# Padding the small on-chip tiles so that every large tile begins at a multiple of 128 bytes

## The chip, the cores and the metric

The kernel runs on one core of a Trainium2 chip. The metric is the device time of one execution in microseconds. A core has a matrix engine (PE, whose loads of the stationary operand are listed apart as PEld), a vector engine (DVE), a scalar engine (ACT), a general engine (POOL) and a sync engine (SP), from whose queue all transfers of this kernel are issued. On-chip memory (SBUF) has 128 partitions; a tile takes the same byte range in each of them, and it is the first byte of this range that the change moves.

## The reference, cut to what matters

The reference is a small transformer in float32: 256 tokens, width 1024. One block has a gated feed-forward, a mixer that joins sparse attention and a gated linear recurrence, and a second gated feed-forward. Two more blocks follow, each with a feed-forward, a mixer (forgetting attention, then latent attention), a feed-forward and a gated embedding. Nearly all work is products of a 256-row activation with weights that are read once:

```python
def swiglu(x, w_gu, w_down):
    gate, up = jnp.split(x @ w_gu, 2, axis=-1)
    return (jax.nn.silu(gate) * up) @ w_down
...
for l in range(DEPTH):
    h = h + 0.5 * swiglu(rms_norm(h, ffn1_norm[l]), ffn1_w_gu[l], ffn1_w_down[l])
    h = h + hybrid_mixer(rms_norm(h, mix_norm[l]), w_in[l], ...)
    h = h + 0.5 * swiglu(rms_norm(h, ffn2_norm[l]), ffn2_w_gu[l], ffn2_w_down[l])
```

## The kernel before, in words

The 256 tokens are two tiles of 128 rows, T = 0 and T = 1. A generator `net(T)` writes out the program of each; `run` steps the two in turn, T = 1 some steps behind, so that one weight serves both soon after each other. The order of instructions on each engine is fixed when the program is built.

**Weights.** `load_unit` issues the transfer of a weight block of 128 x 512 floats into a tile `wr` (6 buffers). ACT rounds it to the PE's fp32r format (L318, tile `w`), and DVE takes the rest that the rounding lost (L319, another tile `w`; 42 buffers in all).

**Products.** `mm3` makes one float32 product from three fp32r matmuls (L347 to L349): the high part of the activation with the high and with the low part of the weight, then the low part of the activation with the high part of the weight. The weight tile `w` is the moving operand and streams through PE (mostly 512 columns); a 128 x 128 piece of the activation (`xh`, `xl` or a working tile `s`) is the stationary operand, and is loaded anew for each matmul. In the rows below `mm<-w,xh` reads: written `mm` in PSUM, moving `w`, stationary `xh`. Two kinds of matmul have it otherwise. At L1198 to L1200 the weight `w` is stationary and the activation `keep` moves, in 256 columns. At L766 the moving operand is a weight again, in plain float32 (two passes, so two instructions, for one product), and the stationary operands are pieces of 30 columns of one tile `s`, each 120 bytes behind the one before.

**Small tiles.** Scalars per row (`col`, a ring of 26 slots; `sc`, `rq`, `gt`) hold statistics and gates. The reciprocal square root of a norm is POOL's power operation (L454 and L544), with a constant column `mhalf` as its exponent.

**Placing.** Tiles are placed in SBUF in the order in which they are first asked for. First come `x0`, the `wr` and the `w` tiles, then the constants, `g1`, `x1`, `mhalf`, and then `xh`, `xl`, the 20 working tiles `s2` (`s` in the rows), `col`, `sc` and the rest. A tile begins at a multiple of 32 bytes, right behind the one before.

Of the kernel before, what the change touches and what calls it, by code (L numbers as in the profile page):

```python
# [11 lines left out]
FT = mybir.dt.float32  # L12
FR = mybir.dt.float32r
# [7 lines left out]
P = 128  # L21
# [242 lines left out]
class Net:  # L264
# [21 lines left out]
        return self.t("keep", [P, n, w], 5, dt)  # L286

    def col(self, n=1):
        return self.t("col", [P, n], 26)

    def pt(self, tag, cols=512):
        self.uid += 1
# [196 lines left out]

    def scales(self, vs):  # L490
        r = self.rstd(vs[0], 1e-6, extra=vs[1])
        sc = self.t("sc", [P, 2], 4)
        self.nc.vector.tensor_scalar(sc[:, 0:1], r, 0.5, None, op0=OP.mult)
        self.nc.vector.tensor_tensor(sc[:, 1:2], r, r, op=OP.mult)
        return sc
# [420 lines left out]
    def nsa_proj(self, T, xT, nsa):  # L916
        nc, sh, c = self.nc, self.sh, self.c
        if T == 0:
            for _ in range(8):
                yield "c1"  # L920
        else:
            yield from self.compress()
        pz = yield from self.dense("nq", xT, 4, 512)
        q = self.s2()
        nc.scalar.activation(q, pz, AF.Copy)
        tp = self.pt("tr")
        for i in range(4):
            self.tr(tp[:, P * i:P * i + P], q[:, P * i:P * i + P])
        nqT = self.s2().rearrange("p (i t) -> p i t", i=4)
        nc.vector.tensor_tensor(nqT, tp.rearrange("p (i t) -> p i t", i=4),  # L930
                                c["qsc"].unsqueeze(2).to_broadcast([P, 4, P]), op=OP.mult)
        nsa["q"] = nqT
        pz = yield from self.dense("vv", xT, 4, 280)
        nc.scalar.activation(sh["nv"][:, T, :], pz[:, 0:256], AF.Copy)
        gt = self.t("gt", [P, 24], 2)
        nc.scalar.activation(gt, pz[:, 256:280], AF.Tanh, scale=0.5)
        nc.vector.tensor_scalar(gt, gt, 0.5, 0.5, op0=OP.mult, op1=OP.add)
        nsa["g"] = gt
# [270 lines left out]
    def mla(self, T, xT, done):  # L1209
        nc, sh = self.nc, self.sh  # L1210
# [3 lines left out]
        with self.tc.high_priority(offset=HP):  # L1214
            q = self.s2()
            nc.vector.tensor_tensor(q[:, 0:384], pz[:, 0:384], self.gain("mla_q_norm_2")[:, 0:384], op=OP.mult)
            ms, junk = self.col(), self.s2()
            nc.scalar.activation(junk[:, 0:384], pz[:, 0:384], AF.Square, scale=384 ** -0.5, accum_out=ms)
            rq = self.rstd(ms, 1e-6, dst=self.t("rq", [P, 1], 2))
            tp = self.pt("tr")  # L1220
            for i in range(3):
                self.tr(tp[:, P * i:P * i + P], q[:, P * i:P * i + P])
            ch, cl = ((self.keep(P, 3, FR) if T == 0 else
                       self.s2(dt=FR)[:, 0:384].rearrange("p (k t) -> p k t", k=3)) for _ in range(2))
            self.split(ch, cl, tp[:, 0:384].rearrange("p (k t) -> p k t", k=3))
# [215 lines left out]


def late(n, nc, sb, a, vec, ct):
    nc.sync.dma_start(ct[:, P:], a["const"][:, P:])
    lf = n.s2()[:, 0:64 * len(LEVELS)]
    nc.sync.dma_start(lf, a["lvl"])
    n.lvl = sb.tile([P, 64 * len(LEVELS)], U8, name="lvl")
    nc.vector.tensor_copy(n.lvl, lf)
    n.c["cpos"] = sb.tile([P, 2, 16], FT, name="cpos")
    nc.sync.dma_start(n.c["cpos"], a["cpos"])  # L1450
    n.w2 = sb.tile([P, 2, 128], FT, name="w2")
    nc.sync.dma_start(n.w2, a["w2"])
    n.bf = sb.tile([P, 16], FT, name="bf")
    o, w = vec["fox_b_f_2"]
    nc.sync.dma_start(n.bf, a["vec"][o:o + w].rearrange("(o w) -> o w", o=1).broadcast_to([P, w]))
    for k in ("hgrn_out_norm", "kv_norm_2", "mla_q_norm_2"):
        o, w = vec[k]
        n.small[k] = sb.tile([P, w], FT, name=k)
        nc.sync.dma_start(n.small[k], a["vec"][o:o + w].rearrange("(o w) -> o w", o=1).broadcast_to([P, w]))
    n.fsel = sb.tile([P, 16], FR, name="fsel")  # L1460
    nc.scalar.activation(n.fsel, n.c["fsel"], AF.Copy)


def build(nc, tc, a, units, offs, coff, vec):
    with tc.tile_pool(name="sb", bufs=1) as sb, tc.tile_pool(name="ps", bufs=1, space=PSUM) as ps:
        n = Net(nc, tc, sb, ps, a, units, offs)
        n.vec = vec
        xs = []
        for T in range(2):
            x = sb.tile([P, D], FT, name=f"x{T}")  # L1470
            xs.append(x)
            if T == 0:
                n.preload(PRE)
                ct = sb.tile([P, a["const"].shape[1]], FT, name="const")
                nc.sync.dma_start(ct[:, 0:P], a["const"][:, 0:P])
                nc.sync.dma_start(x, a["x"][0:P, :])
                n.c["g1"] = sb.tile([P, 8], FT, name="g1")
                nc.sync.dma_start(n.c["g1"], a["g1"])
                n.x, n.small = xs, {}
        for k, (o, w) in coff.items():  # L1480
            n.c[k] = ct[:, o:o + w]
        n.c["mhalf"] = sb.tile([P, 24], FT, name="mhalf")
        nc.gpsimd.memset(n.c["mhalf"], -0.5)
        n.late = lambda: late(n, nc, sb, a, vec, ct)
        n.run()
# [43 lines left out]
```

## Time and profile before

| | |
|---|---|
| median of 3 runs | 1709.43 us (1705.27 to 1710.35) |
| profiled execution, device time | 1710.19 us |
| its span, first to last instruction | 1708.4 us |
| PE busy | 1678.5 us, 98% of the span |
| DVE busy | 1115.4 us, 65% |
| ACT busy | 937.5 us, 55% |
| POOL busy | 23.8 us, 1% |
| mean granted TensorE clock | 0.997 |

All times below are of the profiled execution. Busy time of PE runs from the start of a matmul to its modelled end, and ends overlap the next start, so the pace of PE is read from the starts that follow each other.

### The profile page before, as it was taken

The page shows a single profiled execution, that of the slowest core. Times are in us where ns is not written, and L with a number is a line of the kernel's source. Part 1 is how long each engine was busy: PE and PEld are TensorE (multiplying, and loading weights), DVE is VectorE, ACT ScalarE, POOL GpSimd, SP SyncE. Part 2 cuts the span into 40 slices and gives each one's busy share as a digit, 9 for nine tenths or more (in the row PEclk, how much of TensorE's full clock was granted, in tenths as well). Part 3 has the DMA queues.
Part 4 walks back from the last instruction along what each step waited for, and adds up shares of the span by engine and source line. Part 5 has one row for each costly group of instructions (what it writes and reads, how often), then busy time and mean ns, then how long its engine had stood idle before and what let it go on. Part 6 is the DMA issues. An engine that isn't in the chain of part 4 may idle for free.

```text
span 1708.4 us, 24828 instructions
## 1 busy us (share of the span) xinstructions
PE 1678.5 (98%) x8010; PEld 1346.2 (79%) x8010; DVE 1115.4 (65%) x2308; ACT 937.5 (55%) x1899; POOL 23.8 (1%) x43
## 2 busy tenths in 40 slices
PE   8999999999999999999999999999999999999997
PEld 6888776777888788878887888778888888788876
DVE  6655666666665766567557565785666865766666
ACT  7545665555555555556555555564555774555553
POOL 0000000000000000000000000000000000000000
PEclk9999999999999999999999999999999999999999
DMA  8755554336655566555436555575655633565652
GB/s 270 264 176 171 171 175 125 99 105 191 185 184 174 168 186 188 182 166 158 141 121 198 185 185 184 173 223 165 195 185 163 207 100 99 184 199 185 185 173 74
DMA packets 160402, 292.99 MB, mean 171 GB/s; under 512 B 18192, under 2 KB 27152, under 8 KB 160272
## 3 DMA queue, kind: packets, MB, share of 16 engines
q1 hardware_dynamic: 160272, 291.41, 55.0%
q8 instruction: 63, 1.03, 0.3%
q14 instruction: 67, 0.55, 0.1%
HBM read 290.29 MB, written 1.05 MB: 171 GB/s over the span
## 4 chain that ended last, share of the span: by engine, by line
PE 90%; DVE 4%; ACT 2%; issue 1%; DMA 1%; POOL 1%; SPq 0%; DVEq 0%; POOLq 0%; ACTq 0%
PE mm L347 16%; PE mm L348 16%; PE mm L349 16%; PE a L347 10%; PE a L348 10%; PE a L349 10%; PE tr L357 5%; PE a L766 1%; DMA wr<-wp 1%; DVE x L542 1%; DVE w L319 1%; DVE x L559 1%; PE a L989 1%; PE a L857 1%; PE a L1281 1%
## 5 line engine op out<-in xcount | busy, mean ns | idle before, releaser
L319 DVE TENSOR_TENSOR w<-wr,w 128x512 fp32r<-128x512 f32 (+3 forms) x1058 | 706.7, 680 | 369.6 <-ACT w L318 154.9
L318 ACT ACTIVATE w<-wr 128x512 fp32r<-128x512 f32 (+3 forms) x1058 | 648.7, 622 | 412.8 <-PE mm L348 240.9
L347 PE MATMUL mm<-w,xh 128*128 128x512 f32 (+3 forms) x1200 | 481.2, 401 | 0.0
L348 PE MATMUL mm<-w,xh 128*128 128x512 f32 (+3 forms) x1200 | 470.1, 392 | 0.0
L349 PE MATMUL mm<-w,xl 128*128 128x512 f32 (+3 forms) x1200 | 469.1, 391 | 0.0
L347 PEld LDWEIGHTS mm<-w,xh 128*128 128x128 f32 x1200 | 225.7, 188 | 49.0 <-issue 4.4
L349 PEld LDWEIGHTS mm<-w,xl 128*128 128x128 f32 x1200 | 225.6, 188 | 47.9
L348 PEld LDWEIGHTS mm<-w,xh 128*128 128x128 f32 x1200 | 226.3, 189 | 43.2 <-issue 0.6
L348 PE MATMUL a<-w,s 128*128 128x512 f32 x531 | 211.1, 398 | 0.0
L347 PE MATMUL a<-w,s 128*128 128x512 f32 x531 | 210.5, 396 | 0.5 <-ACT s L352 0.5
L349 PE MATMUL a<-w,s 128*128 128x512 f32 x531 | 209.8, 395 | 0.2 <-DVE s L353 0.2
L347 PEld LDWEIGHTS a<-w,s 128*128 128x128 f32 x531 | 99.6, 188 | 28.7 <-issue 4.1
L347 PE MATMUL a<-w,xh 128*128 128x512 f32 (+2 forms) x304 | 121.0, 399 | 0.8 <-ACT xh L352 0.7
L348 PE MATMUL a<-w,xh 128*128 128x512 f32 (+2 forms) x304 | 119.6, 394 | 0.0
L349 PE MATMUL a<-w,xl 128*128 128x512 f32 (+2 forms) x304 | 119.0, 394 | 0.0
L349 PEld LDWEIGHTS a<-w,s 128*128 128x128 f32 x531 | 99.6, 188 | 23.9 <-DVE s L353 0.6
L348 PEld LDWEIGHTS a<-w,s 128*128 128x128 f32 x531 | 99.7, 188 | 22.9
L352 ACT ACTIVATE s<-tr 128x256 fp32r<-128x256 f32 (+2 forms) x137 | 50.8, 372 | 74.9 <-PE tr L357 74.7
L353 DVE TENSOR_TENSOR s<-tr,s 128x256 fp32r<-128x256 f32 (+2 forms) x137 | 56.5, 413 | 50.8 <-ACT s L352 50.5
L357 PE MATMUL tr<-const,s 128*128 128x128 f32 (+1 forms) x436 | 77.6, 274 | 2.1 <-DVE s L471 1.4
L357 PEld LDWEIGHTS tr<-const,s 128*128 128x128 f32 (+1 forms) x436 | 56.2, 140 | 28.7 <-DVE s L471 2.7
L347 PEld LDWEIGHTS a<-w,xh 128*128 128x128 f32 x304 | 57.5, 189 | 15.6 <-ACT xh L352 3.3
(277 smaller groups left out, 1356.7 us busy)
## 6 DMA issues: line engine op xcount, KB each, us to landing
wr<-wp SPq DMA_DIRECT2D x994, 256.0 KB, 2.7
gb<-vec SPq DMA_DIRECT2D x21, 512.0 KB, 4.0
wr<-wp SPq DMA_DIRECT2D x32, 192.0 KB, 2.4
w<-wp SPq DMA_DIRECT2D x16, 256.0 KB, 4.8
wr<-wp SPq DMA_DIRECT2D x16, 160.0 KB, 2.4
wr<-wp SPq DMA_DIRECT2D x8, 168.0 KB, 2.3
wr<-wp SPq DMA_DIRECT2D x8, 140.0 KB, 2.2
x<-x SPq DMA_DIRECT2D x2, 512.0 KB, 6.2
```

The costliest lines, as they stand in the source:

```text
L318: nc.scalar.activation(hi[:, 0:w], r[:, 0:w], AF.Copy)
L319: nc.vector.tensor_tensor(lo[:, 0:w], r[:, 0:w], hi[:, 0:w].bitcast(FT), op=OP.subtract)
L347: mm(out, xh, wh, start=start, stop=False)
L348: mm(out, xh, wl, start=False, stop=False)
L349: mm(out, xl, wh, start=False, stop=stop)
L352: self.nc.scalar.activation(hi, src, AF.Copy)
L353: self.nc.vector.tensor_tensor(lo, src, hi.bitcast(FT), op=OP.subtract)
L357: self.nc.tensor.transpose(out, src, self.c["ident"][0:n, 0:n])
L542: nc.vector.scalar_tensor_tensor(y[:, cs], y[:, cs], nm, g[:, cs], op0=OP.add, op1=OP.mult)
L559: self.nc.vector.scalar_tensor_tensor(x[:, cs], acc, c, x[:, cs], op0=OP.mult, op1=OP.add, accum_out=s)
L766: nc.tensor.matmul(hp[0:2 * nb, 256 * kv:256 * kv + 256], kbs[kv][:, cc].rearrange("p g b -> p (g b)"), u[i][0], start=cc == 0, stop=cc == 15)
L857: nc.tensor.matmul(ap[:, 64 * h:64 * h + 64], k[:, P * h:P * h + P], dq[:, 64 * h:64 * h + 64], start=True, stop=True)
```

## The change

Small tiles are padded, or become columns of another tile. No instruction is added, removed or moved; addresses change. The ring `col` has 24 slots in place of 26. `g1` and `bf` become columns behind the constants, and `fsel` and `mhalf` share a tile `misc`; `sc`, `gt` and `rq` are padded.

```diff
     def col(self, n=1):
-        return self.t("col", [P, n], 26)
+        return self.t("col", [P, n], 24)
...
-        sc = self.t("sc", [P, 2], 4)
+        sc = self.t("sc", [P, 8], 4)
...
-        gt = self.t("gt", [P, 24], 2)
+        gt = self.t("gt", [P, 32], 2)[:, 0:24]
...
-            rq = self.rstd(ms, 1e-6, dst=self.t("rq", [P, 1], 2))
+            rq = self.rstd(ms, 1e-6, dst=self.t("rq", [P, 16], 2)[:, 0:1])
...
-    nc.sync.dma_start(ct[:, P:], a["const"][:, P:])
+    nc.sync.dma_start(ct[:, P:a["const"].shape[1]], a["const"][:, P:])
...
-    n.bf = sb.tile([P, 16], FT, name="bf")
...
-    n.fsel = sb.tile([P, 16], FR, name="fsel")
+    n.fsel = n.misc[:, 0:16]
...
-                ct = sb.tile([P, a["const"].shape[1]], FT, name="const")
+                nc0 = a["const"].shape[1]
+                ct = sb.tile([P, -(-(nc0 + 24) // 32) * 32], FT, name="const")
...
-                n.c["g1"] = sb.tile([P, 8], FT, name="g1")
+                n.c["g1"] = ct[:, nc0:nc0 + 8]
+                n.bf = ct[:, nc0 + 8:nc0 + 24]
...
-        n.c["mhalf"] = sb.tile([P, 24], FT, name="mhalf")
+        n.misc = sb.tile([P, 32], FR, name="misc")
+        n.c["mhalf"] = n.misc[:, 16:32].bitcast(FT)
```

Where the tiles begin, in bytes past a multiple of 128, as the two programs place them:

| tile | before | after |
|---|---|---|
| `x0`, all `wr`, all `w`, `const` | 0 | 0 |
| `x1` | 64 | 0 |
| `xh`, `xl`, `s2`, `keep`, `gb`, `lvl`, `w2` | 32 | 0 |
| `se`, `pT`, the gains `hgrn_out_norm`, `kv_norm_2`, `mla_q_norm_2` | 96 | 0 |
| `col` slots | 32 or 96 | 0 or 64 |

On SP, the first transfers of the program stand in the same places; `x_61` is `x0`, and `g` in the third row is the tile `g1`. Before:

```order
L1475 DMA const<-const 128x128
L1476 DMA x_61<-x 128x1024
L1478 DMA g_77<-g 128x8
L311 DMA wr_123<-wp 128x512
L311 DMA wr_125<-wp 128x512
```

and in the changed kernel:

```order
L1475 DMA const<-const 128x128
L1476 DMA x_61<-x 128x1024
L1479 DMA const<-g 128x8
L311 DMA wr_122<-wp 128x512
L311 DMA wr_124<-wp 128x512
```

The 4 KB of `g1` go to columns of `const`; nothing has changed its place in the queue.

On POOL, these are the power operations of the second feed-forward of the first block and of the layers behind it, with the engines that each waits for. Before:

```order
L454 TENSOR_TENSOR col_3913<-col_3913,mhalf 128x1 [waits DVE_49]
L454 TENSOR_TENSOR col_4040<-col_4040,mhalf 128x1 [waits DVE_49]
L454 TENSOR_TENSOR col_5779<-col_5779,mhalf 128x1 [waits DVE_49]
L454 TENSOR_TENSOR col_5962<-col_5962,mhalf 128x1 [waits DVE_49]
L544 TENSOR_TENSOR col_7689<-col_7689,mhalf 128x1 [waits DVE_49,Activation_49]
```

and in the changed kernel:

```order
L454 TENSOR_TENSOR col_3910<-col_3910,misc 128x1 [waits DVE_49,Pool_49]
L454 TENSOR_TENSOR col_4037<-col_4037,misc 128x1 [waits DVE_49]
L454 TENSOR_TENSOR col_5776<-col_5776,misc 128x1 [waits DVE_49,Pool_49]
L454 TENSOR_TENSOR col_5959<-col_5959,misc 128x1 [waits DVE_49]
L544 TENSOR_TENSOR col_7686<-col_7686,misc 128x1 [waits DVE_49,Activation_49]
```

The order is the same. Some of the operations name POOL itself as well, for the last use of a `col` slot that now comes round after 24 instead of 26. Over the whole program the waits of PE, DVE and SP are the same one for one; ACT has 4 separate wait instructions fewer and POOL 5 more.

## Rows read from the trace of the kernel before

**Rows 1.** The page: span, then an engine's busy time, share and instructions.

```profile
span 1708.4 us, 24828 instructions
PE 1678.5 (98%) x8010; PEld 1346.2 (79%) x8010; DVE 1115.4 (65%) x2308; ACT 937.5 (55%) x1899; POOL 23.8 (1%) x43
```

**Rows 2.** The page: chain of work that ended last, shares of the span.

```profile
PE 90%; DVE 4%; ACT 2%; issue 1%; DMA 1%; POOL 1%; SPq 0%; DVEq 0%; POOLq 0%; ACTq 0%
```

**Rows 3.** The page's costliest groups: busy us, mean ns, idle before, releaser.

```profile
L347 PE MATMUL mm<-w,xh 128*128 128x512 f32 (+3 forms) x1200 | 481.2, 401 | 0.0
...
L347 PE MATMUL a<-w,s 128*128 128x512 f32 x531 | 210.5, 396 | 0.5 <-ACT s L352 0.5
...
L347 PE MATMUL a<-w,xh 128*128 128x512 f32 (+2 forms) x304 | 121.0, 399 | 0.8 <-ACT xh L352 0.7
```

**Rows 4.** Timeline of PE, 512 columns: start, duration; ten matmuls, first and last.

```profile
400.15 0.39 PE L348 MATMUL mm<-w,xh 128*128 128x512 f32 x1
...
402.25 0.39 PE L348 MATMUL a<-w,xh 128*128 128x512 f32 x1
```

**Rows 5.** Timeline of PE, 320 columns: eight starts, first and last.

```profile
816.67 0.31 PE L349 MATMUL mm<-w,xl 128*128 128x320 f32 x1
...
817.70 0.39 PE L347 MATMUL mm<-w,xh 128*128 128x512 f32 x1
```

**Rows 6.** Timeline of PE, weight stationary, 256 columns: 22 starts, first and last.

```profile
1320.36 0.28 PE L1198 MATMUL mm<-keep,w 128*128 128x256 f32 x1
...
1322.82 0.28 PE L1198 MATMUL a<-keep,w 128*128 128x256 f32 x1
```

**Rows 7.** The chain in order of time: start, length, line, matmuls in it.

```profile
252.13 2.71 PE a L766 x12
...
258.10 2.71 PE a L766 x12
...
1376.92 1.73 PE a L1260 x8
```

**Rows 8.** Loads of stationary operands, by form: busy us, mean ns, idle before.

```profile
L347 PEld LDWEIGHTS mm<-w,xh 128*128 128x128 f32 x1200 | 225.7, 188 | 49.0 <-issue 4.4
...
L357 PEld LDWEIGHTS tr<-const,s 128*128 128x128 f32 x428 | 55.4, 140 | 28.2 <-DVE s L471 2.7 <-issue 1.2 <-ACT s L1246 1.0
L357 PEld LDWEIGHTS tr<-const,se 128*128 128x128 f32 x148 | 18.2, 141 | 12.9 <-ACT se L645 3.9 <-ACT pT L660 3.0 <-ACT se L1014 1.8
```

**Rows 9.** Line 1198 alone: load of the stationary weight, ns min, median, max.

```profile
L1198 PEld LDWEIGHTS mm<-keep,w x24: 186/188/192, 1320.1 to 1395.6; 128*128 128x128 f32 x24
```

**Rows 10.** DVE and ACT by form: busy us, mean ns, idle before, releasers.

```profile
L319 DVE TENSOR_TENSOR w<-wr,w 128x512 fp32r<-128x512 f32 x994 | 674.5, 690 | 348.6 <-PE mm L348 154.8 <-ACT w L318 135.7 <-PE a L348 46.2
...
L353 DVE TENSOR_TENSOR xl<-tr,xh 128x512 fp32r<-128x512 f32 x28 | 19.3, 688 | 5.0 <-ACT xh L352 4.4
...
L318 ACT ACTIVATE w<-wr 128x512 fp32r<-128x512 f32 x994 | 618.0, 631 | 388.1 <-PE mm L348 225.0 <-PE a L348 97.0 <-DMA wr<-wp 17.6
...
L1331 ACT ACTIVATE s<-s 128x512 f32<-128x512 f32 x8 | 5.0, 626 | 4.0 <-DVE s L1330 4.0
```

**Rows 11.** Who waited for whom: us in total, times, longest us.

```profile
POOL col L544 <- DVE col L543: 724.4, 13, 178.7
...
DVE x L547 <- POOL col L544: 6.5, 14, 0.8
```

**Rows 12.** Transfers by line: count, KB each, median us from issue to landing.

```profile
wr<-wp SPq DMA_DIRECT2D x994, 256.0 KB, 2.7
gb<-vec SPq DMA_DIRECT2D x21, 512.0 KB, 4.0
...
x<-x SPq DMA_DIRECT2D x2, 512.0 KB, 6.2
```

**Rows 13.** One stretch: us, busy PE, PEld, DVE, ACT, POOL (instructions), clock, DMA, GB/s.

```profile
344.88:351.71 6.83, 6.83 (x29) 6.34 (x29) 0.89 (x3) 1.21 (x7) 0.00 (x0) 0.50 0.00 0
```

## The prediction

> **What bounds the kernel now.** I read the page first. PE is busy for 1678.5 of 1708.4 us, and no other engine for more than 65% of the span [rows 1]. The chain of work that ended last lies on PE for 90% [rows 2]. The costliest matmul groups have next to no idle time ahead of them [rows 3]: PE is not waiting for operands, it is working at its own pace. So the change can gain or lose much only if it alters the pace of a matmul, or makes PE wait.
>
> The pace is read from starts in the timeline of PE. Nine steps of 512 columns take 402.25 - 400.15 = 2.10 us, so 233.3 ns each [rows 4]. The granted clock is 0.997, nearly always the upper level of 2.4 GHz, and 512 columns at one per cycle would take 213.3 ns. So 20.0 ns of each such matmul is something else. Of these matmuls there are 3 x (1200 + 531 + 304) = 6,105 [rows 3], and 6,105 x 20.0 ns = 122 us is the largest thing in this profile that placing could touch. Whether it does is the question.
>
> **The change part by part.** No engine has an instruction more, less or elsewhere, so there are no added or removed operations to cost. What is left are three kinds of effect.
>
> *Stationary operands move from 32 bytes past a multiple of 128 to a multiple.* The moving weights `w` began at a multiple before and still do, so for the 6,105 matmuls only the load of `xh`, `xl` or `s` changes. Such a load takes 188 ns [rows 8] and runs beside the matmul before it, which paces at 233.3 ns: cover of 45 ns. Without that cover, a matmul would be paced by its load. The loads themselves show no trace of the offset. At L1198 the stationary operand is a weight, which does begin at a multiple of 128, and its load takes 188 ns as well [rows 9]. Transposes load pieces of `s` (offset 32) in 140 ns and of `se` (offset 96) in 141 ns [rows 8].
>
> The pace says the same in three ways. First, a theft by the load should be the same for every width, because each load is 128 columns wide; but the time over one column per cycle grows with the width. At 320 columns seven steps take 1.03 us, 147.1 ns each [rows 5], against 133.3 ns: 13.8 ns over. At 256 columns 21 steps take 2.46 us, 117.1 ns each [rows 6], against 106.7 ns: 10.5 ns over. At 512 it is 20.0 ns. Divided by the width this is 0.043, 0.041 and 0.039 ns per column: one law. Second, the 256-column matmuls obey it with everything exchanged: there the stationary operand begins at a multiple of 128 and the moving one (`keep`) 32 bytes past it. Third, L766 loads pieces that begin at 32, 24, 16, 8, 0 and 120 bytes past a multiple in the run at 252.13 us, and at 96, 88, 80, 72, 64 and 56 in the run at 258.10 us. Both runs of 12 take 2.71 us [rows 7].
>
> The bounds: a straight line through 320 and 512 columns leaves (13.8 - 320 x (20.0 - 13.8) / 192) = 3.5 ns that don't grow with the width; through 256 and 512 columns it leaves 1.0 ns. So at best a load takes 3.5 ns from each matmul and the new place gives all of it back: 6,105 x 3.5 ns = 21 us. At worst the new place, where load and stream begin at the same offset, costs as much again: 21 us more. I take zero, since the direct comparisons [rows 7 to 9] show no difference.
>
> *Operands of DVE and ACT move.* On DVE the subtraction of 512 columns takes 690 ns with all SBUF operands at a multiple of 128 (`w`, `wr`), and 688 ns with both 32 bytes past it (`xl`, `xh`). On ACT the copy takes 631 ns from `wr` to `w` and a function from `s` to `s` 626 ns [rows 10]. Nothing to win; and a few ns there would only lengthen the idle time of engines that PE hides. Bounds: the difference of 5 ns on ACT, on all 1,000 or so such operations, is 5 us of ACT time, of which PE sees none while these groups have hundreds of us of idle time ahead of them [rows 10].
>
> *Transfers and waits.* The weight tiles don't move, so 994 of the large transfers are as before. `gb` (21 transfers, 4.0 us) and `x1` land at other offsets [rows 12]; `gb` is asked for a stage ahead. If each of the 21 took 1 us less or more, nothing ends later. The `col` ring of 24 makes a few POOL operations name POOL's own earlier work. POOL waits for DVE for 724.4 us in 13 waits, and DVE then waits for POOL for 0.8 us at most [rows 11]. A slot comes round after 24 requests, so its last reader is long done. Behind a waiting POOL operation stand only later power operations; if one wait did bite, DVE's second pass of the norm (L547) would be late, then the transposes on PE. Half a microsecond in each of the 14 waits would be 7 us; I take zero. `g1` keeps its place in the queue.
>
> The sum is 0 us on the profiled execution's own 1710.19 us (span 1708.4 us and 1.8 us around it). That execution lies 0.8 us above the median of the three runs, so I predict the median itself, 1709.4 us, rounded to 1709.
>
> **The rivals.** "Measurable" is a difference of over 0.3%, 5.1 us, about what the three runs of before spread.
>
> *Slower: loads and streams collide.* With every offset 0, a load and the stream beside it ask for the same part of a 128-byte line at once, which 32 bytes kept apart. For it: this pairing hasn't occurred in the fp32r matmuls. Against: at L1260 moving and stationary operand are both tiles `s`, at the same offset, and eight matmuls of 256 columns take 1.73 us, 216 ns each, no more than the 226 ns of L766, whose offsets differ [rows 7]. DVE reads `w` and `wr` at the same offset without loss [rows 10]. Price up to 21 us, so 1731 us; it decides from 5.1 us / 6,105 = 0.8 ns per matmul. Chance 0.11.
>
> *Faster a little: the loads do take something.* The constant part of 1.0 to 3.5 ns comes back in part or whole: 6 to 21 us, 1688 to 1703 us. For it: the line through 320 and 512. Against: the loads are as long at either offset. Chance 0.15.
>
> *Faster by much: the 20 ns are the price of any operand off a multiple.* The 256-column matmuls too have one operand off it, the moving one; so the law could be the same because in each kind of matmul one of the two is misplaced. No row shows an fp32r matmul with both at a multiple. If so, 122 us go: 1587 us. Against: a late load would have to cost in proportion to the columns that stream past it, and by the same factor as a late stream. Chance 0.05. The Trainium skill (TensorE: Matmul & The Clock Gate, section "Wait — 56ns, not 53.3ns?") gives 215.7 ns from start to start for 512 columns at the upper level of the clock. The trace shows 233.3 ns, so by the page 17.6 ns of each matmul are a loss, and if the placing were its cause the time would be, as an estimate from that page, 6,105 x 17.6 ns = 107 us less, 1602 us. The page doesn't say what operands its matmuls had.
>
> *The clock.* For 6.83 us the granted clock was 0.50, the lower level, after a stretch of short matmuls, and PE was busy throughout [rows 13]. If slightly moved waits removed this stretch, or made another, that is about half of it, 3.4 us either way: below what can be told, but it adds to the spread. A chance of 0.02 that several such stretches make it measurably slower.
>
> **How the numbers follow.** No measurable change: 0.67, the likeliest, with its own range of 1704 to 1715. Faster: 0.15 + 0.05 = 0.20. Slower: 0.11 + 0.02 = 0.13. The range takes in the likeliest case and most of the small gain down to 1691, and a little of the loss, up to 1716: about 0.67 + 0.12 + 0.02 = 0.81.
>
> **What would show it right or wrong.** Right: in the profile after, the starts of 512-column matmuls follow at 233.3 ns, loads take 188 ns, 512-column DVE subtractions 690 and 688 ns, and PE is busy for 98%. If the 512-column step falls, the placing paces PE and I am wrong at the law of the widths; a step of about 213 ns would be the large gain, 230 to 232 ns the small one. If the step grows, they collide. If the step is unchanged but the time isn't, look at the waits of ACT and POOL for `col` slots, and at where the clock was at its lower level.

## The result, and the profile after

The change made the kernel faster: a median of 1680.54 us (1677.74 to 1685.55, 4 runs) against 1709.89 us (1705.27 to 1710.51, 4 runs) beside it, a ratio of 0.9839 with a 95% interval of 0.9824 to 0.9854. That is 29 us, where no measurable change was forecast, and below the range of 1691 to 1716. The changed kernel's four executions spread with their mean granted clock: 1677.74 us at 0.999, 1678.79 at 0.997, 1682.29 at 0.995 and 1685.55 at 0.994. The profiled execution took 1682.29 us with a span of 1680.5 us, 27.9 us less than the 1708.4 us of [rows 1].

The page after: the span, the engines' busy time, the chain that ended last, the matmul groups and loads, and two transfers.

```profile
span 1680.5 us, 24829 instructions
...
PE 1649.4 (98%) x8010; PEld 1345.9 (80%) x8010; DVE 1110.6 (66%) x2308; ACT 936.7 (56%) x1899; POOL 23.5 (1%) x43
...
PE 87%; DVE 6%; ACT 2%; DMA 2%; issue 2%; POOL 1%; SPq 0%; DVEq 0%; POOLq 0%; ACTq 0%
...
L347 PE MATMUL mm<-w,xh 128*128 128x512 f32 (+3 forms) x1200 | 477.5, 398 | 0.3 <-DVE s L584 0.3
...
L347 PEld LDWEIGHTS mm<-w,xh 128*128 128x128 f32 x1200 | 226.0, 188 | 43.9 <-issue 4.4
...
L347 PE MATMUL a<-w,s 128*128 128x512 f32 x531 | 208.1, 392 | 0.5 <-ACT s L352 0.5
...
wr<-wp SPq DMA_DIRECT2D x994, 256.0 KB, 2.7
gb<-vec SPq DMA_DIRECT2D x21, 512.0 KB, 4.3
```

PE is still the bound: 98% busy, and 87% of the chain. But it is busy for 29.1 us less than in [rows 1] with the same 8010 instructions. So it isn't waiting less, it is working faster. The stationary loads take 188 ns as in [rows 8], and next to no idle time stands ahead of the matmuls, as in [rows 3].

The timeline of PE after, first and last matmul of three runs: 512 columns, 320 columns (up to the next matmul of 512), and 256 columns at L1198 to L1200.

```profile
393.73 0.39 PE L348 MATMUL mm<-w,xh 128*128 128x512 f32 x1
...
395.77 0.39 PE L348 MATMUL a<-w,xh 128*128 128x512 f32 x1
...
795.33 0.30 PE L347 MATMUL mm<-w,xh 128*128 128x320 f32 x1
...
796.21 0.39 PE L347 MATMUL mm<-w,xh 128*128 128x512 f32 x1
...
1298.77 0.28 PE L1198 MATMUL mm<-keep,w 128*128 128x256 f32 x1
...
1301.28 0.28 PE L1198 MATMUL a<-keep,w 128*128 128x256 f32 x1
```

At 512 columns nine steps take 2.04 us: 226.7 ns each, against 233.3 ns in [rows 4]. At 320 columns six steps take 0.88 us: 146.7 ns each, as before (147.1 ns in [rows 5], read to a hundredth of a us). At 256 columns 21 steps take 2.51 us: 119.5 ns each, slower than the 117.1 ns in [rows 6]. So the excess over one column per cycle no longer grows with the width: it is now 13.4 ns at 512 columns, 13.4 at 320 and 12.9 at 256, where it was 20.0, 13.8 and 10.5.

The span's gain is in the 512-column matmuls. This table sums the times from one start to the next, over the whole trace, by the width of an fp32r matmul with another fp32r matmul behind it; the second row has what else follows 512 columns, and the rows of the transposes and of L766 count every one:

```
from start to start          count   before us   after us   difference
512 columns, then fp32r       5631      1341.1     1312.7        -28.4
512 columns, then others       284        81.8       83.9         +2.0
320 columns                               14.2       14.2          0.0
336 columns                                7.5        7.5          0.0
384 columns                               34.2       34.0         -0.2
256 columns                               12.4       12.6         +0.2
transposes (L357)                         73.4       73.0         -0.4
L766                                      15.4       15.4          0.0
span                                    1708.4     1680.5        -27.9
```

In the second row something else follows, mostly a transpose; 2.0 us are lost again there. 5,590 of the 5,631 steps of the first row lead to a further 512-column matmul, and these alone give 28.3 us.

Little else has changed. DVE and ACT by form, waits, the chain, and two stretches at the lower level of the clock (columns as in [rows 10], [rows 11], [rows 7] and [rows 13]):

```profile
L319 DVE TENSOR_TENSOR w<-wr,w 128x512 fp32r<-128x512 f32 x994 | 670.8, 689 | 334.7 <-ACT w L318 152.5 <-PE mm L348 146.8 <-PE a L348 26.2
...
L318 ACT ACTIVATE w<-wr 128x512 fp32r<-128x512 f32 x994 | 618.3, 631 | 371.9 <-PE mm L348 219.9 <-PE a L348 91.2 <-DMA wr<-wp 18.5
```

```profile
POOL col L544 <- DVE col L543: 981.8, 14, 174.5
...
DVE x L547 <- POOL col L544: 6.6, 14, 0.8
```

```profile
246.55 2.71 PE a L766 x12
...
252.50 2.71 PE a L766 x12
...
1354.73 1.73 PE a L1260 x8
```

```profile
338.91:345.74 6.83, 6.83 (x30) 6.42 (x30) 1.06 (x3) 1.05 (x6) 0.00 (x0) 0.50 0.00 0
779.23:782.65 3.42, 3.42 (x10) 2.63 (x9) 1.49 (x7) 1.43 (x7) 0.00 (x0) 0.50 0.10 18
```

DVE takes 689 and ACT 631 ns, DVE waits for POOL in 14 waits of at most 0.8 us, and the runs at L766 and L1260 last 2.71 and 1.73 us. The stretch at clock 0.50 of [rows 13] is there again, and a second one, of 3.42 us. If what ran there takes half as long at the upper level, that costs this execution some 1.7 us, so the clock gave nothing.

### The profile page after: what moved, and what is told of

Read it like the earlier page. It is cut to its first block, busy times and chain, and to the rows that moved or that the text cites. A ratio compares the mean times of both kernels' runs of the same rounds, so it can differ in the third digit from the quotient of the medians.

```text
span 1680.5 us, 24829 instructions
## 1 busy us (share of the span) xinstructions
PE 1649.4 (98%) x8010; PEld 1345.9 (80%) x8010; DVE 1110.6 (66%) x2308; ACT 936.7 (56%) x1899; POOL 23.5 (1%) x43
## 4 chain that ended last, share of the span: by engine, by line
PE 87%; DVE 6%; ACT 2%; DMA 2%; issue 2%; POOL 1%; SPq 0%; DVEq 0%; POOLq 0%; ACTq 0%
PE mm L347 16%; PE mm L349 15%; PE mm L348 15%; PE a L347 10%; PE a L348 10%; PE a L349 10%; PE tr L357 4%; DMA wr<-wp 1%; DVE w L319 1%; DVE x L542 1%; PE a L766 1%; ACT w L318 1%; DVE x L559 1%; DVE x L547 1%; PE a L989 1%
## 5 line engine op out<-in xcount | busy, mean ns | idle before, releaser
L349 PE MATMUL mm<-w,xl 128*128 128x512 f32 (+3 forms) x1200 | 465.3, 388 | 0.0
L348 PE MATMUL mm<-w,xh 128*128 128x512 f32 (+3 forms) x1200 | 464.7, 387 | 0.0
L349 PEld LDWEIGHTS mm<-w,xl 128*128 128x128 f32 x1200 | 225.9, 188 | 43.3
L348 PEld LDWEIGHTS mm<-w,xh 128*128 128x128 f32 x1200 | 226.6, 189 | 38.9 <-issue 0.6
L347 PE MATMUL a<-w,s 128*128 128x512 f32 x531 | 208.1, 392 | 0.5 <-ACT s L352 0.5
L348 PE MATMUL a<-w,s 128*128 128x512 f32 x531 | 207.5, 391 | 0.0
L349 PE MATMUL a<-w,s 128*128 128x512 f32 x531 | 207.3, 391 | 0.1
L348 PE MATMUL a<-w,xh 128*128 128x512 f32 (+2 forms) x304 | 118.3, 389 | 0.0
L349 PE MATMUL a<-w,xl 128*128 128x512 f32 (+2 forms) x304 | 117.2, 388 | 0.0
L349 PEld LDWEIGHTS a<-w,s 128*128 128x128 f32 x531 | 99.6, 188 | 21.1 <-DVE s L353 0.6
L348 PEld LDWEIGHTS a<-w,s 128*128 128x128 f32 x531 | 99.7, 188 | 19.9
L353 DVE TENSOR_TENSOR s<-tr,s 128x256 fp32r<-128x256 f32 (+2 forms) x137 | 56.4, 413 | 47.6 <-ACT s L352 47.3
```

What stands on the lines that cost most here:

```text
L347: mm(out, xh, wh, start=start, stop=False)
L348: mm(out, xh, wl, start=False, stop=False)
L349: mm(out, xl, wh, start=False, stop=stop)
L353: self.nc.vector.tensor_tensor(lo, src, hi.bitcast(FT), op=OP.subtract)
```

## The experiments

The time went into the pace of the 512-column matmuls. What makes the pace? Four theories were put against each other:

- **A**: the stationary piece has a good place of its own, a multiple of 64 bytes.
- **B**: the same with a multiple of 128 bytes, as the change is made.
- **C**: what counts is the *distance*: the start of the stationary piece that is loaded, less the start of the moving tile that streams meanwhile. It was first thought of modulo 128, and 0 as good.
- **D**: it is not the large tiles at all, but the small ones (`col`, `sc`, `gt`, `rq`, `g1`).

Since `mm3` runs its matmuls in threes, the pace is given as the mean time of three steps, counted over some 1,480 undisturbed threes of 512 columns in each trace (before 700.0 ns, after 682.0 ns). Undisturbed are those of under 720 ns from the first start to the start of a 512-column matmul behind the third. Places are taken from the built program. Before, `w` began at 128 and `xh`, `xl` and `s` at 32, modulo 256: a distance of 160 (32 modulo 128). After, all four are at 128: a distance of 0. All experiments but the last are edits of the changed kernel.

### The stationary operands moved by 32, 64 and 96 bytes

An unused tile behind `misc` moves all that is placed later, `xh`, `xl` and `s` among it, while `wr` and `w` stay. In st32:

```diff
         nc.gpsimd.memset(n.c["mhalf"], -0.5)
+        sb.tile([P, 8], FT, name="gap")
```

In st64 and st96 the tile has 16 and 24 columns (64 and 96 bytes).

> The changed kernel with one unused tile of 32 bytes behind misc, so that xh, xl, the working tiles s and all behind them begin 32 bytes past a multiple of 128 again, while w and wr stay at a multiple; the small tiles stay as changed. If only the place of the stationary operands matters (theories A, B and C), three 512-column matmuls take 700 ns again (233.3 ns each) and the time is 1709 us within 5. If the small tiles or the ring of 24 col slots had made the gain (theory D), the step stays at 226.7 ns and the time at 1681 us.

> The same with 64 bytes. Theory A (the stationary operand has to begin at a multiple of 64 bytes: a load of 512 bytes then touches 8 pieces of 64 bytes and not 9): 226.7 ns and 1681 us. Theory B (at a multiple of 128 bytes): 233.3 ns and 1709 us. Theory C (what counts is the distance between the places of the stationary and of the moving operand, 0 being good): 233.3 ns and 1709 us.

> The same with 96 bytes. Theories A, B and C all say 233.3 ns and 1709 us; if the step is something else, none of the three is right as it stands.

| kernel | distance | time, us | ratio to before | three steps, ns |
|---|---|---|---|---|
| st32 | 32 | 1706.51 (1703.12 to 1708.72) | 0.9991 [0.998, 1.0001] | 699.5 |
| st64 | 64 | 1708.38 (1704.86 to 1710.3) | 0.9999 [0.9989, 1.0009] | 700.1 |
| st96 | 96 | 1709.95 (1707.6 to 1711.62) | 1.0003 [0.9993, 1.0012] | 702.5 |

32 unused bytes take the gain away, though every small tile keeps its padding and `col` its 24 slots: D has nothing left to stand on here. st64 loses it too: its stationary tiles are at multiples of 64, so A falls. The page of st64, its first rows, and then the timeline of PE in st32 and in st64, first and last of 24 matmuls of 512 columns each:

```profile
span 1706.6 us, 24829 instructions
...
PE 1679.1 (98%) x8010; PEld 1347.4 (79%) x8010; DVE 1115.8 (65%) x2308; ACT 937.8 (55%) x1899; POOL 23.5 (1%) x43
```

```profile
999.73 0.40 PE L347 MATMUL mm<-w,xh 128*128 128x512 f32 x1
...
1005.10 0.40 PE L349 MATMUL a<-w,s 128*128 128x512 f32 x1
```

```profile
999.62 0.40 PE L348 MATMUL mm<-w,xh 128*128 128x512 f32 x1
...
1004.99 0.39 PE L347 MATMUL mm<-w,xh 128*128 128x512 f32 x1
```

23 steps take 5.37 us in both: 233.5 ns each, and PE is busy for 1679.1 us, as before the change.

### Everything moved off the multiple, and one kind of tile alone

In all32 the unused tile of 32 bytes stands ahead of the first `wr`, so every large tile but `x0` begins 32 bytes past a multiple of 128, and the distance stays 0:

```diff
             if T == 0:
+                sb.tile([P, 8], FT, name="gap")
                 n.preload(PRE)
```

In w32 it stands between `wr` and `w`: `wr` stays, all else moves, with a distance of 0:

```diff
     def wt(self, dt=FT):
+        if not self.gap:
+            self.gap = True
+            self.sb.tile([P, 8], FT, name="gap2")
         return self.t("w", [P, HALF], N_W, dt)
```

In wr32 there are both, 32 bytes ahead of `wr` and 96 behind it (and 22 slots of `col` to make room), so that `wr` alone is off. all32b is all32 once more.

> The changed kernel with the unused tile of 32 bytes ahead of wr, so that every large tile, the moving w too, begins 32 bytes past a multiple of 128. Theory C (distance between the two): the distance is 0 as in the changed kernel, so 226.7 ns and 1681 us. Theories A and B (place of the stationary operand by itself): 233.3 ns and 1709 us, or more if a misplaced moving operand costs something of its own. DVE and ACT at 690 and 631 ns for 512 columns by all of them.

> The changed kernel with the unused tile of 32 bytes between wr and w: wr stays at a multiple of 128, and w, xh, xl, s and the rest all begin 32 bytes past one. Theory C (the distance between the places of stationary and moving operand counts, not either place): three 512-column matmuls take 680 ns and the time is 1681 us within 5. Theories A and B (the stationary operand's own place): 700 ns and 1709 us. It also repeats the run with every tile moved, two executions of which took over 3800 us, with the weights' landing place wr left alone: if transfers to a place 32 bytes past a multiple were the cause of those, no such execution comes here.

> Only the landing tiles wr are moved: 32 bytes ahead of wr and 96 behind it, so that w, xh, xl and s keep their distance and stay at a multiple of 128 (the ring col gives 128 bytes for it and has 22 slots). Theory C: 680 ns for three matmuls, 1681 us. If transfers to 32 bytes past a multiple can be slow, executions far above 1700 us come here; if they were an accident of the other run, none.

> The kernel with all large tiles 32 bytes off, a second time: 1681 us by the theory of the distance, since the distance is 0. Two of its four executions took over 3800 us, and moving wr alone or w and the rest alone brought no such execution. If they belong to the kernel, they come again; if they were an accident of that chip at that time, all are near 1681 us.

| kernel | off the multiple | time, us | ratio to before | three steps, ns |
|---|---|---|---|---|
| all32 | all | 1678.0, 1686.37, 3840.57, 4230.05 | none | 682.3 |
| all32b | all | 1682.21 (1679.1 to 1683.94) | 0.9848 [0.9833, 0.9862] | 682.3 |
| w32 | all but `wr` | 1679.85 (1677.45 to 1681.67) | 0.9826 [0.9805, 0.9848] | 682.3 |
| wr32 | `wr` alone | 1680.94 (1677.73 to 1685.11) | 0.9836 [0.9814, 0.9859] | 682.0 |

Two of the four executions of all32 took more than twice as long, so it has no ratio; the same program sent again as all32b had no such execution in four, and why it happened stays open. The traces of all four agree on 682 ns. In all32, all32b and w32 no operand of `mm3` begins at a multiple of 128, and the whole gain is there: B falls, and C is left. The closest pair is st32 and w32. In both, `xh`, `xl` and `s` begin at 160, modulo 256; of the operands of `mm3` only `w` differs, 128 in st32 and 160 in w32, and with it the pace, 699.5 and 682.3 ns. The page of w32, and its timeline of PE (in w32, L351 to L353 are the three matmuls of `mm3`):

```profile
span 1678.6 us, 24829 instructions
...
PE 1647.5 (98%) x8010; PEld 1343.3 (80%) x8010; DVE 1111.5 (66%) x2308; ACT 939.7 (56%) x1899; POOL 23.6 (1%) x43
```

```profile
999.74 0.39 PE L352 MATMUL mm<-w,xh 128*128 128x512 f32 x1
...
1004.95 0.39 PE L351 MATMUL a<-w,s 128*128 128x512 f32 x1
```

23 steps take 5.21 us: 226.5 ns each. wr32 also shows that the place of `wr` doesn't matter; only DVE and ACT read it.

### Modulo what? A distance of 128 and one of 256

The same edit as st32, with an unused tile of 32 columns (128 bytes) and 22 slots of `col` in dist128, and of 64 columns (256 bytes) and 20 slots in dist256. In both, every large tile begins at a multiple of 128, just as in the changed kernel.

> The unused tile of 128 bytes behind misc (again with 22 col slots): stationary operands begin 128 bytes past the place of the moving ones, taken modulo 512, where the changed kernel has 0. If the distance counts modulo 128 (theory C as it stands): 680 ns and 1681 us. If it counts modulo 256 or 512: 700 ns and 1709 us, and the multiple of 128 was good by luck.

> The unused tile behind misc has 256 bytes (20 col slots pay for it): every stationary operand begins 256 bytes from the place of the moving one, taken modulo 512. If the distance counts modulo 256, as the run with the working tiles spread out suggests: 680 ns for three matmuls, 1681 us within 5. If modulo 512: 700 ns, 1709 us.

| kernel | distance | time, us | ratio to before | three steps, ns |
|---|---|---|---|---|
| dist128 | 128 | 1705.65 (1700.29 to 1710.1) | 0.9985 [0.9971, 1.0] | 697.9 |
| dist256 | 256 | 1679.24 (1679.13 to 1679.32) | 0.9832 [0.9816, 0.9849] | 682.4 |

The timeline of PE in dist128, 19 matmuls of 512 columns, and in dist256, 24:

```profile
999.78 0.39 PE L349 MATMUL a<-w,s 128*128 128x512 f32 x1
...
1003.96 0.39 PE L349 MATMUL a<-w,s 128*128 128x512 f32 x1
```

```profile
999.79 0.39 PE L348 MATMUL mm<-w,xh 128*128 128x512 f32 x1
...
1005.00 0.39 PE L347 MATMUL a<-w,s 128*128 128x512 f32 x1
```

18 steps of 4.18 us are 232.2 ns each, 23 of 5.21 us are 226.5 ns. So C was wrong in its modulus: a distance of 128 loses nearly the whole gain, one of 256 keeps it. And what the change says of itself, multiples of 128 bytes, isn't enough: dist128 has them. That the changed kernel has a distance of 0 modulo 256 is where its sizes happened to end. Its own trace shows the same at a distance of 128, which 74 of its undisturbed steps still have, mostly where a piece of `keep` is loaded: 231.6 ns on average, against 227.8 ns of the 5,224 at distance 0.

### All distances in one kernel

In sweep0 each of the 20 tiles `s` is 32 bytes longer, so that they stand at distances 0, 32, 64 and so on; in sweep16 the used part also begins 16 bytes later. One `w` tile fewer makes room (41). The rows of `s` in one run are then a comparison at sixteen distances:

```diff
-N_W = 42
+N_W = 41
...
-        return self.t("s2", [P, cols], N_S2, dt)
+        return self.t("s2", [P, cols + 8], N_S2, dt)[:, 0:cols]
```

In sweep16 the last line ends in `[:, 4:cols + 4]`.

> The 20 working tiles s are 32 bytes longer each (one weight tile w fewer, 41, pays for it), so that they begin at 20 places in steps of 32 bytes, and every distance from the moving weight up to 608 bytes occurs in one run; xh and xl stay at distance 0. Theory C modulo 128: matmuls with s take 680 ns for three where the distance is 0, 128, 256, 384 or 512, and 700 ns at the 15 others; modulo 512 only at 0 and 512. Matmuls with xh and xl stay at 680 ns. The time lies between 1681 and 1709 us: a quarter of the 1,593 matmuls with s keeps the gain, so about 1681 + 0.75 x 1593 x 6 ns = 1688 us, less sure for the weight tile that is missing.

> The working tiles spread over 20 places again, now 16 bytes further: distances 16, 48, 80 and so on. If only an exact multiple of 256 is good: 695 to 704 ns for three matmuls with s at every distance. If the good place is wider than one step: 680 to 690 ns at 16 or 240. Matmuls with xh at 680 ns. If one distance gives less than 680 ns, a better version than the changed kernel can be built.

One execution each: 1685.58 and 1682.96 us. These threes are the ones in which all pieces, that of the next product too, are of `s` and at one distance:

```
distance, modulo 256   three steps, ns: mean (median)   count
  0                    684.1 (680)                         33
 16                    688.4 (680)                         33
 32                    696.2 (695)                         34
 48                    700.5 (701)                         34
 64                    700.9 (702)                         49
 80                    696.0 (695)                         49
 96                    699.7 (700)                         41
112                    699.7 (700)                         41
128                    697.8 (697)                         21
144                    686.4 (680)                         21
160                    700.3 (700)                         19
176                    691.6 (691)                         19
192                    690.9 (687)                         31
208                    693.3 (692)                         31
224                    699.9 (700)                         42
240                    683.2 (680)                         42
```

The best three take 680 ns at the distances 240, 0 and 16, and at 144; from 32 to 128, at 160 and at 224 nearly all of the loss is there; from 176 to 208 half of it. No distance is faster than 680 ns. Threes with `xh` and `xl`, which stay at a distance of 0, take 684.4 and 684.1 ns in these two runs, some 2 ns more than after the change. The old distance of 160 was about the worst that there is.

### Who pays: a bad place for `xl` alone

In xl32 only `xl` is at a distance of 32, between two unused tiles (again with 41 `w` tiles). In `mm3` the piece of `xl` is loaded for the third matmul (L349), so while the second one (L348) streams. In this kernel the lines of `mm3` are unchanged.

```diff
         hi = self.t("xh", [P, n, P], 4, FR)
+        self.t("gap", [P, 8], 1)
         lo = self.t("xl", [P, n, P], 4, FR)
+        self.t("gap2", [P, 56], 1)
```

> Only the four tiles xl lie 32 bytes off, xh and s stay at distance 0 (one weight tile w fewer pays for it). Of the three matmuls of a product with xh and xl, the second streams while the piece of xl is loaded, and the third uses it. If the loss falls on the matmul that streams during the load, the start of the third follows that of the second by about 7 ns more than in the changed kernel, and three take 687 ns; if on the one that uses the operand, the gap behind the third grows; if one bad operand upsets all three, 695 to 700 ns. Products with s stay at 680 ns. Time: 1,504 products with xh and xl by 7 ns are 10 us, so about 1691 us, or 1708 us if all three lose.

One execution: 1693.44 us, about half of the loss. Threes with `s` take 684.9 ns, threes with `xh` and `xl` 697.7 ns, where 687 were expected for one slower matmul of the three. In its trace the steps from one 512-column matmul of `mm3` to the next take 18.1 us more than after the change; the span grew by 11.2 us only, in part since only 3.42 us, not 6.83 and 3.42, lay at clock 0.50 amid the work. The page of xl32, groups of `mm3`:

```profile
L347 PE MATMUL mm<-w,xh 128*128 128x512 f32 (+3 forms) x1200 | 479.9, 400 | 0.0
L348 PE MATMUL mm<-w,xh 128*128 128x512 f32 (+3 forms) x1200 | 473.1, 394 | 0.0
L349 PE MATMUL mm<-w,xl 128*128 128x512 f32 (+3 forms) x1200 | 463.9, 387 | 0.0
...
L349 PEld LDWEIGHTS mm<-w,xl 128*128 128x128 f32 x1200 | 225.6, 188 | 47.0 <-issue 0.7
```

L349, whose own stationary piece is the misplaced one, takes 387 ns on average, as all of `mm3` but the first does after the change. L348 takes 394 ns: it is the matmul that streams while the misplaced piece is loaded. From start to start the three of an `xh` and `xl` product take 231.6, 237.6 and 228.6 ns, against 227.2, 227.6 and 227.5 ns after the change: 10.0 of 15.4 ns lie on the one that streams beside the load, 4.4 ns on the one ahead of it. The load of the misplaced piece stays at 188 ns, and ends on average 46 ns before the third matmul starts (37 ns after the change). So the price shows in the step of the matmul that streams beside the load, not in the load's length, and a matmul whose own piece is misplaced pays next to nothing. What this does not explain: one misplaced load of three costs 15.4 ns, nearly as much as three of them (17.7 ns, 682.3 to 700.0), and 4.4 ns of it lie ahead of the load. By the distance alone it would be a third, some 6 ns.

### The kernel before, with nothing but 96 unused bytes

If C holds modulo 256, the kernel before needs none of the change. An unused tile of 96 bytes behind `mhalf` takes `xh`, `xl` and `s` from 32 to 128, modulo 256, so to a distance of 0. One slot of `col` goes to make room; all other small tiles stay as they were.

```diff
-        return self.t("col", [P, n], 26)
+        return self.t("col", [P, n], 25)
...
         nc.gpsimd.memset(n.c["mhalf"], -0.5)
+        sb.tile([P, 24], FT, name="gap")
```

> The kernel before, with none of the edits of the change but one unused tile of 96 bytes behind mhalf (the ring col gives one slot for it, 25 in place of 26). The stationary operands then begin 0 bytes, modulo 256, from the place of the moving ones, and no small tile is padded: x1, keep, gb, the gains and the col slots stay where the change would not leave them. Theory C modulo 256: 680 ns for three matmuls and the whole gain, 1681 us within 5. If some of the gain comes from the other large tiles or from the small ones: between 1681 and 1709 us.

It took 1679.84 us (1677.88 to 1681.72), a ratio of 0.9839 [0.982, 0.9859]: all of the gain. Three steps take 682.4 ns. The page of before96, and its timeline of PE, 24 matmuls:

```profile
span 1679.2 us, 24836 instructions
...
PE 1647.8 (98%) x8010; PEld 1343.8 (80%) x8010; DVE 1111.2 (66%) x2308; ACT 936.7 (56%) x1899; POOL 23.5 (1%) x43
```

```profile
999.70 0.39 PE L349 MATMUL mm<-w,xl 128*128 128x512 f32 x1
...
1004.91 0.39 PE L348 MATMUL mm<-w,xh 128*128 128x512 f32 x1
```

23 steps of 5.21 us, 226.5 ns each. D falls for good, since not one small tile is padded here. No version beats the changed kernel beyond the intervals: dist256 (0.9832), before96 (0.9839) and the change (0.9839) are one time.

## Why the prediction was wrong, by its own steps

**What bounds the kernel: right.** PE at its own pace is the bound, and 512-column matmuls are where placing could touch. That the 20.0 ns over one column per cycle are "something else" was the right thing to ask about.

**The law of the widths: the step that failed.** The prediction said that "a theft by the load should be the same for every width", and found instead an excess of about 0.04 ns per column. Both halves were wrong. The excess is not proportional: after the change it is 13.3 ns per matmul at 512, 336, 320 and 256 columns alike (steady threes of 680, 460, 440 and 360 ns). And what the load takes is not the same for every width: by moving from distance 160 to 0, three steps of 512 columns became 20 ns shorter, those of 384 columns some 7 ns (most took 527 to 532 ns, now 520 to 524 ns), those of 336 and 320 no shorter. The 256-column matmuls, which have other operands, went from a distance of 224 to one of 128 and became up to 10 ns longer (350 to 360). So 20.0, 13.8 and 10.5 ns were three different cases that lay on a line by accident. The straight line through two of them, and with it the bound of 3.5 ns, measured nothing; 6.7 ns per steady matmul were there. The forecast took even less than that bound, zero, on the strength of the comparisons of [rows 7 to 9], where 28.4 us came. (Its count of 6,105 matmuls of 512 columns is off by little: 384 of them, under the "+ forms" of [rows 3], have fewer columns, and with the groups left out there the trace has 5,916.)

**"With everything exchanged": a comparison that wasn't one.** The 256-column matmuls were read as proof that the place of the stationary operand doesn't matter. They had another distance (224) and another width, so they could not stand for the others. Over the kernels here their threes take 360 ns where the distance is 0 (wr32 and both sweeps), mostly 360 at 128, and 351 to 355 at the other five that occur: at this width equal starts are not the fast case.

**Loads of 188 ns at either offset: a true row, a wrong inference.** They are 188 ns in every kernel here, fast or slow. But xl32 shows that most of the price is in the matmul that streams beside the load. Nor was there a "cover of 45 ns" without which "a matmul would be paced by its load": at 320 and 256 columns the steps of 147.1 and 117.1 ns [rows 5], [rows 6] are shorter than the load of 188 ns, and successive loads overlap, as these two of the kernel before do:

```profile
1320.60 0.19 PEld L1198 LDWEIGHTS mm<-keep,w 128*128 128x128 f32 x1
1320.72 0.19 PEld L1199 LDWEIGHTS mm<-keep,w 128*128 128x128 f32 x1
```

The equal runs at L766 and L1260 [rows 7] are true as well, and stayed equal, but those are 256-column matmuls in plain float32, and say nothing of 512 columns of fp32r.

**DVE, ACT, transfers, waits, `col`, clock: right.** DVE 689 for 690 ns, ACT 631 for 631 ns, `gb` 4.3 for 4.0 us, DVE's longest wait for POOL 0.8 us. st32 has all of these edits and none of the gain.

**The rivals.** *Faster a little: the loads do take something* (0.15) was the right mechanism with its term mis-sized: at most 3.5 ns each and 21 us, where a steady matmul gave back 6.7 ns, and all 5,631 steps from a 512-column matmul to the next fp32r matmul 28.4 us, 5.0 ns on average. The average is lower since the first matmuls behind a break don't reach the pace at once (below). *Slower: loads and streams collide* (0.11) had the two disturbing each other by their places, which is so, but with the wrong sign: at equal starts they go fast, and at the 32 bytes that were thought to keep them apart they go slow (st32: 699.5 ns). *Faster by much* (0.05) didn't come: no kernel has a 512-column step under 226.7 ns in a steady three, so 13.3 of the 20.0 ns are there at the best distance too. The 215.7 ns that the Trainium skill gives (TensorE: Matmul & The Clock Gate, section "Wait — 56ns, not 53.3ns?") were not reached by any placing tried here; the trace doesn't agree with that figure for these matmuls.

What stays open: why the period is 256 bytes, why 144 is good, why one misplaced load of three costs nearly the price of three, and why 256 columns go the other way. The runs show the price by distance, not the part of the chip in which the load and the stream meet.

## What to carry to other kernels

Where fp32r matmuls of 512 columns follow each other with a fresh load for each, place the stationary tile and the tile that streams during its load at the same start modulo 256 bytes, and read the built addresses rather than trust a multiple of 128. At 320 and 336 columns nothing was won, and at 256 columns equal starts were the slower case. Read the pace from starts, in runs of one shape and one pair of tiles, and don't fit a law through shapes whose places differ as well. A suspicion about placing costs one unused tile to test: a few bytes of padding that move one kind of tile, and nothing else.

## What was not expected of the hardware

- The pace of 512-column fp32r matmuls, each with its own load, depends on the distance of stationary and moving operand modulo 256 bytes: 226.7 ns at 0, 233.3 ns at 160, with the good places 240, 0, 16 and 144 of the sixteen tried. The load itself takes 188 ns at all of them.
- The loss depends on the width: 6.7 ns at 512 columns, some 2 ns at 384, none at 336 and 320, between the distances 160 and 0. At 256 columns, with the weight stationary, distance 0 is 3 ns per matmul slower than 224 (360 and 351 ns for three).
- Loads of 188 ns overlap: at 256 columns they start some 117 ns apart, so a load longer than the step doesn't set the pace.
- After the change 1,248 of 1,480 threes take exactly 680 ns, and nearly all others stand behind a break. Counting threes that follow each other directly, of the 204 first ones of a run 180 take over 684 ns (691.9 ns on average), of the second 30 in 145, of the sixth and later none in 777. The pace falls into step only after a while. Before, the first threes took 699.9 ns and the later ones 700, with no such start.
